# The recurrence's small inverse as its own chain, a few rows at a time, its first step tied behind eight VectorE instructions; u and v in one tile a head

## Chip, core and metric

The kernel runs on one core of a Trainium2 chip. The metric is the device time of one execution in microseconds (us), taken as the median of several runs. A profiled execution gives the trace that this document reads. The engines are called as the profile does: PE (TensorE, matrix products), PEld (its weight loads), DVE (VectorE), ACT (ScalarE), POOL (GpSimd) and SP (SyncE, which issues nearly all transfers here).

## What is computed

Two stacks of two layers each. A layer of the first stack has a mixer of three branches (a multi-scale pool, a differential attention, a two-way recurrence), gates, an output product and an MLP; the second stack has three kinds of attention. The change concerns only the recurrence of the first stack:

```python
def wkv7_scan(r, w, k, v, kk, a, reverse):
    def step(state, inp):
        r_t, w_t, k_t, v_t, kk_t, a_t = inp
        sa = einsum('bhij,bhj->bhi', state, -kk_t)
        state = (state * w_t[:, :, None, :] + sa[..., None] * (kk_t * a_t)[:, :, None, :]
                 + v_t[..., None] * k_t[:, :, None, :])
        return state, einsum('bhij,bhj->bhi', state, r_t)
    ...
y = direction(0, False) + direction(1, True)
```

There are 8 heads of 64 features, 512 steps and two directions. The kernel computes the scan in chunks of 64 steps. Within a chunk the steps hang together by a triangular 64x64 matrix for each head, direction and chunk, which has to be inverted.

## The kernel before

**Stages.** In each of the two layers of the first stack, `mixer` interleaves four generators. `rwkv_prepare` works through 4 pairs of heads; for each pair `rwkv_pair` makes the projections, and for each half of the sequence `rwkv_stage` makes the decayed keys and the masked products `scr` (L746 on PE, L748 on DVE), the transposed keys `bt` and the tile `uv`. So there are 8 stages a layer, 16 in all, and each ends in one inverse; they are called chain 1 to chain 16 here. `rwkv_recur` runs the chunks with what the stages left. `others` makes the pool and attention branches, and `gates` the gate products. Most of PE's time goes to products of the last two and of the projections: each is 24 matmuls 128x512 at L95 (`mm3`), whose weights are loaded to `wraw` and split by ACT (`whi`, L73) and DVE (`wlo`, L75).

**The inverse.** The four 32x32 diagonal blocks go by SP from `scr` to DRAM (`nd`, L782) and back, spread over the partitions, into `cN` (L789). Then come 31 steps of forward substitution on DVE, each a product into `cT` (L793) and a subtraction from `cX` (L795), 62 instructions in a row of dependences, and one negation (L796). `cX` goes to DRAM (`nx`, L797) and from there to its place in `scr` (L800). `rwkv_merge` adds the off-diagonal block: DVE transposes to `xz` (L813), PE multiplies twice (L816 and L823) with a copy by ACT between (L818). `cN`, `cX` and `cT` have one buffer each.

**The chunks.** `rwkv_chunks` makes for each chunk `px` (L837, L845), `xs` (ACT), `pu` (L854), then u, whose upper half ACT writes (L856) and whose lower half DVE writes (L857) into the same tile `uv`, then `pu` again (L862) and the next state `hist` (DVE, L869 or L872).

**What sets the order.** `Weave` holds the generators as chains with a priority and a time at which they are due, and lets the due one with the smallest number go on to its next `yield`, whose figures say how much PE time the piece is reckoned to fill and how long the chain then rests (1.8 times the second figure). The recurrence has priority 0, the preparation 1, the attention pieces 2, the other branches 3, the gates 4. The whole inverse is written out at the end of `rwkv_stage` in one piece; the merge is added as a chain of priority 0.2, due 60 of the planner's microseconds later:

```python
wv.add(0.2, self.rwkv_merge(rp, 2 * p + g, st, blocks, (sc, ar, bt, uv, pe)), 60.0)
```

A scheduler of the build then sets the final order on each engine's queue from what is written and from its own reckoning; that order is shown below where it matters. Each queue is worked off in that order.

Of the kernel before, what the change touches and what calls it, by code (L numbers as in the profile page):

```python
# [10 lines left out]
AF = mybir.ActivationFunctionType  # L11
ALU = mybir.AluOpType
# [3 lines left out]
P = 128  # L16
# [13 lines left out]
class B:  # L30
# [20 lines left out]
    def dump(self, name, ap):  # L51
        if self.dbg is not None and name in self.dbg:
            self.nc.gpsimd.dma_start(self.dbg[name], ap)


# [152 lines left out]
class First:  # L208
# [476 lines left out]
    def rwkv_stage(self, l, p, g, rp, wag, krkk, vv, st, wv):  # L685


        b, nc, pr = self.b, self.nc, self.pr
# [17 lines left out]
        for d in range(2):  # L706
            i = 4 * d + p
# [50 lines left out]
        yield 1.0, 0.0  # L758
        uv = b.t(rp, [P, 2, 2, 4, 64], "uv", bufs=2)
        nc.gpsimd.memset(uv[0:64, 0], 0.0)  # L760
        nc.gpsimd.memset(uv[64:P, 1], 0.0)
        ps = b.t(pr, [P, 2, 4, 64], "sc")
# [6 lines left out]
        for hh in range(2):  # L769
            nc.scalar.activation(out=uv[hss[1 - hh], hh], in_=ps[hss[1 - hh]], func=AF.Copy)  # L770
        yield 0.9, 0.0
# [8 lines left out]
        for h in range(2):  # L780
            for q in range(2):
                nc.sync.dma_start(nd[8 * h : 8 * h + 8, q].rearrange("n s t -> s n t"), blocks(h, q, q))  # L782
        N = b.t(rp, [P, 32, 32], "cN")
        X = b.t(rp, [P, 8, 32], "cX")
        tmp = b.t(rp, [P, 8, 32], "cT")
        nc.gpsimd.memset(X, 0.0)
        for e in range(4):
            nc.gpsimd.memset(X[32 * e : 32 * e + 32].rearrange("p i t -> p (i t)")[:, e::36], -1.0)
        nc.sync.dma_start(N.rearrange("p s t -> p (s t)"),  # L789
                          nd.rearrange("n q s t -> (n q) (s t)").unsqueeze(0).to_broadcast([4, 32, 1024]))  # L790
        for s_ in range(31):
            ni, nt = s_ // 4 + 1, 31 - s_
            nc.vector.tensor_tensor(out=tmp[:, :ni, :nt], in0=X[:, :ni, s_ : s_ + 1].to_broadcast([P, ni, nt]),  # L793
                                    in1=N[:, s_ : s_ + 1, s_ + 1 :].to_broadcast([P, ni, nt]), op=ALU.mult)
            nc.vector.tensor_tensor(out=X[:, :ni, s_ + 1 :], in0=X[:, :ni, s_ + 1 :], in1=tmp[:, :ni, :nt], op=ALU.subtract)  # L795
        nc.vector.tensor_scalar(out=X, in0=X, scalar1=-1.0, scalar2=None, op0=ALU.mult)  # L796
        nc.sync.dma_start(nx.rearrange("n q i e t -> e (n q) i t"), X)  # L797
        for h in range(2):
            for q in range(2):
                nc.sync.dma_start(blocks(h, q, q), nx[8 * h : 8 * h + 8, q].rearrange("n i e t -> (i e) n t"))  # L800
        wv.add(0.2, self.rwkv_merge(rp, 2 * p + g, st, blocks, (sc, ar, bt, uv, pe)), 60.0)

    def rwkv_merge(self, rp, i, st, blocks, parts):
# [8 lines left out]
        for h in range(2):  # L812
            nc.vector.transpose(out=xz[lo[h]], in_=blocks(h, 0, 0))  # L813
        for n in range(8):
# [14 lines left out]
    def rwkv_chunks(self, rp, g, hist, sc, ar, bt, uv, pe):  # L829
# [4 lines left out]
        for d in range(2):  # L834
            for c in range(4):
                for hh, hs in enumerate(hss):
                    nc.tensor.matmul(px[hs, d, c, :], lhsT=sc[:, d, c, hh, 0:64], rhs=uv[:, hh, d, c, :],  # L837
                                     start=(d == 0 and c == 0), stop=True, skip_group_check=True)
        yield 1.0, 0.0
        for c in range(4):  # L840
# [11 lines left out]
            for d in range(2):  # L852
                for hh, hs in enumerate(hss):
                    nc.tensor.matmul(pu[hs, 0, d, :], lhsT=sc[hs, d, c, hh, 0:64], rhs=xs[hs, d, :],  # L854
                                     start=(d == 0), stop=True, skip_group_check=True)
            nc.scalar.activation(out=uv[0:64, 0, :, c, :], in_=pu[0:64, 0], func=AF.Copy, scale=-1.0)  # L856
            nc.vector.tensor_scalar(out=uv[64:P, 1, :, c, :], in0=pu[64:P, 0], scalar1=-1.0, scalar2=None, op0=ALU.mult)  # L857
            yield 0.35, 0.7

            for d in range(2):  # L860
                for hh, hs in enumerate(hss):
                    nc.tensor.matmul(pu[hs, 1, d, :], lhsT=bt[:, hh, d, c, :], rhs=uv[:, hh, d, c, :], start=False, stop=True, skip_group_check=True)  # L862
            if cc:
# [11 lines left out]
    def rwkv_out(self, g, i, hist, y, st, sc, ar, bt, uv, pe):  # L875

        nc, b, pr = self.nc, self.b, self.pr
        hss = [slice(64 * hh, 64 * hh + 64) for hh in range(2)]
        for d in range(2):
            py = b.t(pr, [P, 4, 64], "sc")  # L880
            for c in range(4):
                for hh, hs in enumerate(hss):
                    nc.tensor.matmul(py[hs, c, :], lhsT=uv[:, hh, d, c, :], rhs=sc[:, d, c, hh, 64:P],
                                     start=(c == 0), stop=True, skip_group_check=True)
            for c in range(4):
                cc = 4 * g + c
                if cc:
                    for hs in hss:
                        nc.tensor.matmul(py[hs, c, :], lhsT=hist[hs, cc - 1, d, :], rhs=ar[hs, d, c, 64:P], start=False, stop=True, skip_group_check=True)
            nc.scalar.activation(out=y[:, d, 256 * g : 256 * g + 256].rearrange("p (c t) -> p c t", t=64), in_=py, func=AF.Copy)  # L890
            if not d:
                yield 1.1, 0.0
        st["done", i] = 1
        yield 1.1, 0.0
# [919 lines left out]
```

## Time and profile before

| | before |
|---|---|
| median of 3 runs | 3659.78 us (3654.95 to 3664.11) |
| profiled execution, its own time | 3664.09 us |
| span of its trace | 3662.3 us |
| PE busy | 3432.6 us, 94% of the span |
| DVE busy | 1888.0 us, 52% |
| ACT, POOL busy | 1221.1 us (33%), 552.2 us (15%) |
| mean granted PE clock | 0.968 |
| mixer of layer 0, mixer of layer 1 | about 90 to 700 us, 1200 to 1850 us |

A row of the page or of a wait table reads engine, line, operation, what it writes and reads, its form and how often, and behind the bar busy time and idle time ahead of it with what ended that. A busy PE is not a PE at its peak, since its matmuls overlap: a matmul 128x512 shows a duration of some 0.39 us while the next one starts 0.23 us after it.

### The profile page before, as it was taken

The page shows a single profiled execution, that of the slowest core. Times are in us where ns is not written, and L with a number is a line of the kernel's source. Part 1 is how long each engine was busy: PE and PEld are TensorE (multiplying, and loading weights), DVE is VectorE, ACT ScalarE, POOL GpSimd, SP SyncE. Part 2 cuts the span into 40 slices and gives each one's busy share as a digit, 9 for nine tenths or more (in the row PEclk, how much of TensorE's full clock was granted, in tenths as well). Part 3 has the DMA queues.
Part 4 walks back from the last instruction along what each step waited for, and adds up shares of the span by engine and source line. Part 5 has one row for each costly group of instructions (what it writes and reads, how often), then busy time and mean ns, then how long its engine had stood idle before and what let it go on. Part 6 is the DMA issues. An engine that isn't in the chain of part 4 may idle for free. (4 is left out here: it accounts for less than half of the span.)

```text
span 3662.3 us, 56248 instructions
## 1 busy us (share of the span) xinstructions
PE 3432.6 (94%) x22346; PEld 2748.1 (75%) x22346; DVE 1888.0 (52%) x4547; ACT 1221.1 (33%) x2339; POOL 552.2 (15%) x660
## 2 busy tenths in 40 slices
PE   7898989989999998989989999899999999999998
PEld 5666767678887666666768888888989978787777
DVE  6547666452235556566544234565465344645634
ACT  2233433222223333333222223344333234443423
POOL 2111211122201211111022210210000111100011
PEclk9899999999999998989999999999999999999999
DMA  5332223333333232222342335222222322222232
GB/s 176 84 83 73 62 70 95 101 119 98 92 94 128 82 92 68 65 69 69 104 142 70 98 92 147 48 42 62 63 68 70 87 73 59 54 57 70 70 92 92
DMA packets 471831, 309.37 MB, mean 84 GB/s; under 512 B 105084, under 2 KB 433796, under 8 KB 471568
## 3 DMA queue, kind: packets, MB, share of 16 engines
q1 hardware_dynamic: 470992, 303.68, 29.7%
q8 instruction: 176, 2.88, 0.3%
q0 software_dynamic: 576, 2.10, 0.1%
q14 instruction: 87, 0.71, 0.1%
HBM read 280.76 MB, written 24.95 MB: 83 GB/s over the span
## 5 line engine op out<-in xcount | busy, mean ns | idle before, releaser
L95 PE MATMUL mm<-xh,whi 128*128 128x512 f32 (+2 forms) x3024 | 1007.8, 364 | 32.9 <-DVE cX L795 26.4
L95 PE MATMUL mm<-xh,wlo 128*128 128x512 f32 (+2 forms) x3024 | 973.2, 353 | 8.5 <-DVE wlo L75 7.2
L95 PE MATMUL mm<-xl,whi 128*128 128x512 f32 (+2 forms) x3024 | 973.9, 353 | 0.0
L75 DVE TENSOR_TENSOR wlo<-wraw,whi 128x1024 fp32r<-128x1024 f32 (+3 forms) x454 | 529.0, 1165 | 607.9 <-ACT whi L73 593.4
L73 ACT ACTIVATE whi<-wraw 128x1024 fp32r<-128x1024 f32 (+2 forms) x466 | 452.5, 971 | 1107.1 <-PE mm L95 846.2
L95 PEld LDWEIGHTS mm<-xh,whi 128*128 128x128 f32 x3024 | 543.4, 192 | 134.9 <-issue 51.4
L95 PEld LDWEIGHTS mm<-xh,wlo 128*128 128x128 f32 x3024 | 540.4, 192 | 89.7 <-DVE wlo L75 10.9
L95 PEld LDWEIGHTS mm<-xl,whi 128*128 128x128 f32 x3024 | 541.2, 192 | 74.9 <-issue 8.9
L1276 ACT ACTIVATE s<-s,nm 128x256 f32<-128x256 f32 (+5 forms) x216 | 116.2, 539 | 184.8 <-DVE nm L1274 182.9
L793 DVE TENSOR_TENSOR cT<-cX,cN 128x60 f32<-128x60 f32 (+24 forms) x496 | 113.3, 229 | 114.2 <-DMA cN<-nd 88.8
L95 PE MATMUL mm<-yh,whi 128*128 128x512 f32 (+1 forms) x480 | 160.1, 368 | 7.4 <-ACT yh L108 4.1
L1054 PE MATMUL b<-whi,hh 128*128 128x512 f32 x416 | 164.6, 396 | 0.4 <-DVE PT L314 0.4
L1054 PE MATMUL b<-whi,hl 128*128 128x512 f32 x416 | 164.5, 395 | 0.0
L1054 PE MATMUL b<-wlo,hh 128*128 128x512 f32 x416 | 164.5, 395 | 0.0
L95 PE MATMUL mm<-yl,whi 128*128 128x512 f32 (+1 forms) x480 | 156.1, 358 | 3.3 <-DVE yl L109 3.3
L95 PE MATMUL mm<-yh,wlo 128*128 128x512 f32 (+1 forms) x480 | 154.0, 353 | 0.0
L1042 POOL TENSOR_TENSOR hid<-r 128x512 f32<-128x512 f32 x64 | 102.2, 1597 | 268.9 <-ACT r L1041 268.9
L109 DVE TENSOR_TENSOR hl<-hid,hh 128x512 fp32r<-128x512 f32 x64 | 43.3, 691 | 164.1 <-ACT hh L108 164.1
L795 DVE TENSOR_TENSOR cX<-cX,cT 128x60 f32<-128x60 f32 (+24 forms) x496 | 113.4, 229 | 10.6
L95 PEld LDWEIGHTS mm<-yh,whi 128*128 128x128 f32 x480 | 83.7, 189 | 28.2 <-ACT yh L108 7.0
L108 ACT ACTIVATE hh<-hid 128x512 fp32r<-128x512 f32 x64 | 39.3, 629 | 191.2 <-PE b L1054 184.4
L1310 DVE TENSOR_TENSOR y<-at,zs 128x128 f32<-128x128 f32 (+2 forms) x120 | 31.2, 263 | 138.9 <-PE at L1307 138.2
(377 smaller groups left out, 5108.9 us busy)
## 6 DMA issues: line engine op xcount, KB each, us to landing
wraw<-in_w_in_dram SPq DMA_DIRECT2D x228, 512.0 KB
wraw<-in_w_up_dram SPq DMA_DIRECT2D x64, 512.0 KB
wraw<-in_w_down_dram SPq DMA_DIRECT2D x64, 512.0 KB
wraw<-in_w_branch_dram SPq DMA_DIRECT2D x48, 512.0 KB
wraw<-in_w_out_dram SPq DMA_DIRECT2D x32, 512.0 KB
g<-acc SPq DMA_DIRECT2D x32, 256.0 KB
cN<-nd SPq DMA_DIRECT2D x16, 512.0 KB
th<-g SPq DMA_DIRECT2D x32, 256.0 KB
```

The lines of the kernel that those rows point to most:

```text
L73: self.nc.scalar.activation(out=wh, in_=rv, func=AF.Copy)
L75: eng.tensor_tensor(out=wl, in0=rv, in1=wh.bitcast(F32), op=ALU.subtract)
L95: self.nc.tensor.matmul(ps, lhsT=wt[:, k, :], rhs=xt[:, k, cs], start=(start and k == 0 and j == 0), stop=(k == nk - 1 and j == 2), skip_g ...
L108: nc.scalar.activation(out=hi, in_=ps, func=AF.Copy)
L109: nc.vector.tensor_tensor(out=lo, in0=ps, in1=hi.bitcast(F32), op=ALU.subtract)
L793: nc.vector.tensor_tensor(out=tmp[:, :ni, :nt], in0=X[:, :ni, s_ : s_ + 1].to_broadcast([P, ni, nt]), in1=N[:, s_ : s_ + 1, s_ + 1 :].to_b ...
L795: nc.vector.tensor_tensor(out=X[:, :ni, s_ + 1 :], in0=X[:, :ni, s_ + 1 :], in1=tmp[:, :ni, :nt], op=ALU.subtract)
L1042: nc.gpsimd.tensor_tensor(out=hidden(m), in0=r, in1=r, op=ALU.mult)
L1054: nc.tensor.matmul(ps[tt, n], lhsT=x[:, tk], rhs=y[:, 0, ns], start=(k == 0 and j == 0), stop=(k == FF - 1 and j == 2))
L1276: nc.scalar.activation(out=ss[i][:n, :nk], in_=ss[i][:n, :nk], func=AF.Exp, bias=nm[:n, i : i + 1], accum_out=sm[:n, i : i + 1])
L1310: nc.vector.tensor_tensor(out=y[:, c], in0=o[:, c.start - P * j : nq], in1=zs[:, c], op=ALU.mult)
```

## The change

1. The inverse leaves `rwkv_stage` and becomes the generator `rwkv_inverse`, a chain of its own with priority 0.2, due 17 of the planner's microseconds after the stage. It yields after every fourth step (rest 1.4), so that it is written out in eight pieces.
2. A stage waits with its `cN` transfer until the chain before it is written out (`("inv", i - 1)`); then it writes the transfer and adds the chain.
3. `b.pin` ties an instruction behind the last eight that were written for the same engine before it (an order alone, no semaphore). The first step of each chain is tied so, and the two transposes of each merge.
4. The merge is due 9 after the chain's end, where it was 60 after the stage's.
5. `uv` is two tiles, one a head, so that ACT's and DVE's halves of u are no longer writes to one tile.

The instructions are the same in kind and number on every engine; only their order and their waits differ.

```diff
+    def pin(self, ins, n=8):
+        found = 0
+        for i in reversed(self.nc.cur_bb.bb.instructions):
+            if i is not ins.ins and i.engine == ins.ins.engine:
+                self.tc.add_manual_dep(
+                    ins.ins, i.name, mybir.DependencyInfo(mybir.DependencyClass.NoSync, mybir.DependencyReason.DATA), reason="pin"
+                )
+                found += 1
+                if found == n:
+                    break
...
-        uv = b.t(rp, [P, 2, 2, 4, 64], "uv", bufs=2)
+        uv = [b.t(rp, [P, 2, 4, 64], f"uv{hh}", bufs=2) for hh in range(2)]
...
+        i = 2 * p + g
+        if i:
+            yield lambda: ("inv", i - 1) in st
         N = b.t(rp, [P, 32, 32], "cN")
+        nc.sync.dma_start(N.rearrange("p s t -> p (s t)"),
+                          nd.rearrange("n q s t -> (n q) (s t)").unsqueeze(0).to_broadcast([4, 32, 1024]))
+        wv.add(0.2, self.rwkv_inverse(rp, i, st, wv, blocks, N, nx, (sc, ar, bt, uv, pe)), 17.0)
+
+    def rwkv_inverse(self, rp, i, st, wv, blocks, N, nx, parts):
...
+            if s_ == 0:
+                b.pin(ins)
             nc.vector.tensor_tensor(out=X[:, :ni, s_ + 1 :], in0=X[:, :ni, s_ + 1 :], in1=tmp[:, :ni, :nt], op=ALU.subtract)
+            if s_ % 4 == 3:
+                yield 0.0, 1.4
...
-        wv.add(0.2, self.rwkv_merge(rp, 2 * p + g, st, blocks, (sc, ar, bt, uv, pe)), 60.0)
+        st["inv", i] = 1
+        wv.add(0.2, self.rwkv_merge(rp, i, st, blocks, parts), 9.0)
...
-            nc.vector.transpose(out=xz[lo[h]], in_=blocks(h, 0, 0))
+            b.pin(nc.vector.transpose(out=xz[lo[h]], in_=blocks(h, 0, 0)))
...
-            nc.scalar.activation(out=uv[0:64, 0, :, c, :], in_=pu[0:64, 0], func=AF.Copy, scale=-1.0)
-            nc.vector.tensor_scalar(out=uv[64:P, 1, :, c, :], in0=pu[64:P, 0], scalar1=-1.0, scalar2=None, op0=ALU.mult)
+            nc.scalar.activation(out=uv[0][0:64, :, c, :], in_=pu[0:64, 0], func=AF.Copy, scale=-1.0)
+            nc.vector.tensor_scalar(out=uv[1][64:P, :, c, :], in0=pu[64:P, 0], scalar1=-1.0, scalar2=None, op0=ALU.mult)
```

What moves is seen on two queues. The first place is DVE's queue in layer 0 from the end of chain 1 (the negation of `cX`) to the start of chain 2 (`cT` written 128x31). The number behind a name tells one buffer's use from another's; `zk` is a projection on its way out of PSUM. Before:

```order
L796 TENSOR_SCALAR cX_840<-cX_840 128x256
L75 TENSOR_TENSOR wlo_1282<-wraw_1279,whi_1281 128x1024
L390 SCALAR_TENSOR_TENSOR zk_1240<-mm_1215,PT_76,zk_1240 128x511
L793 TENSOR_TENSOR cT_1112<-cX_1111,cN_1110 128x31
L392 SCALAR_TENSOR_TENSOR zk_1240<-mm_1215,PT_76,zk_1240 128x511
L795 TENSOR_TENSOR cX_1111<-cX_1111,cT_1112 128x31
L813 STREAM_TRANSPOSE xz_1482<-scr_634 32x256
```

The same place after the change, where the lines have moved down (L796 is now L820, L75 is L87, L390 and L392 are L402 and L404, L510 is L522, L793 is L813, L795 is L817, L813 is L838, L857 is L882, L872 is L897). The negation that ends chain 1 stands three rows ahead of the first row shown, with two more `wlo` between:

```order
L87 TENSOR_TENSOR wlo_1363<-wraw_1360,whi_1362 128x1024
L522 SCALAR_TENSOR_TENSOR s_229_1299<-s_228_1295,s_224_1285 128x512
L87 TENSOR_TENSOR wlo_1485<-wraw_1482,whi_1484 128x1024
L402 SCALAR_TENSOR_TENSOR zk_1334<-mm_1309,PT_76,zk_1334 128x511
L404 SCALAR_TENSOR_TENSOR zk_1334<-mm_1309,PT_76,zk_1334 128x511
L838 STREAM_TRANSPOSE xz_1338<-scr_634 32x256 x2
L87 TENSOR_TENSOR wlo_1566<-wraw_1563,whi_1565 128x1024
L402 SCALAR_TENSOR_TENSOR zr_1457<-mm_1366,PT_76,zr_1457 128x511
L404 SCALAR_TENSOR_TENSOR zr_1457<-mm_1366,PT_76,zr_1457 128x511
L882 TENSOR_SCALAR uv_151_806<-pu_1417 64x2x64
L897 TENSOR_SCALAR hist_272<-pu_1417,pe_655 128x64 x2
L813 TENSOR_TENSOR cT_1437<-cX_1436,cN_1262 128x31
```

Between the end of one chain and the start of the next stood two instructions and stand now fifteen, among them five `wlo`, the merge's transposes and the first chunk of the recurrence.

The second place is PE's queue at the merge of chain 2: the merge's first product (`sc` from `xz` and `scr`), what stands between, and its second. Before:

```order
L816 MATMUL sc_1671<-xz_1670,scr_916 32x32 x16
L515 MATMUL at_1692<-s_258_1530,pw_1532 128x512
L854 MATMUL pu_1697<-xs_1668,scr_634 64x64 x4
L95 MATMUL mm_1637<-xh_69,whi_1633 128x512
L95 MATMUL mm_1637<-xl_70,whi_1633 128x512
L95 MATMUL mm_1637<-xh_69,wlo_1634 128x512
L95 MATMUL mm_1637<-xh_69,whi_1633 128x512
L95 MATMUL mm_1637<-xl_70,whi_1633 128x512
L95 MATMUL mm_1637<-xh_69,wlo_1634 128x512
L862 MATMUL pu_1697<-uv_805,bt_784 64x64 x4
L823 MATMUL sc_1722<-scr_916,xz_1670 32x32 x16
```

After the change (L816 is now L841, L823 is L848, L95 is L107, L422 is L434, L447 is L459); the first of the merge's sixteen 32x32 products stands two rows ahead of the first row shown:

```order
L107 MATMUL mm_1865<-xh_69,whi_1861 128x512
L107 MATMUL mm_1865<-xl_70,whi_1861 128x512
L107 MATMUL mm_1865<-xh_69,wlo_1862 128x512
L107 MATMUL mm_1865<-xh_69,whi_1861 128x512
L434 MATMUL at_1852<-ident_63,yo_1828 128x128 x4
L459 MATMUL at_1929<-kh_1723,qh_1625 128x512
L459 MATMUL at_1929<-kl_1724,qh_1625 128x512
L841 MATMUL sc_1831<-xz_1830,scr_842 32x32 x15
L459 MATMUL at_1929<-kh_1723,ql_1626 128x512
L107 MATMUL mm_1865<-xl_70,whi_1861 128x512
L459 MATMUL at_1930<-kh_1723,qh_1625 128x512
L848 MATMUL sc_1872<-scr_842,xz_1830 32x32 x16
```

One product of the merge now stands ahead of the other fifteen, with a few large ones between, and three large matmuls stand between the merge's two halves, where two groups of the recurrence and seven large ones stood.

## Rows read from the trace of the kernel before

**Rows 1.** The page's first part, the whole execution: busy time, share of span, instructions.

```profile
PE 3432.6 (94%) x22346; PEld 2748.1 (75%) x22346; DVE 1888.0 (52%) x4547; ACT 1221.1 (33%) x2339; POOL 552.2 (15%) x660
```

**Rows 2.** Busy time by stretch, us: PE, PEld, DVE, ACT, POOL, then PEclk, DMA share, GB/s.

```profile
90.00:700.00 610.00, 549.43 (x4355) 407.38 (x4354) 365.05 (x1067) 205.19 (x418) 98.75 (x169) 0.94 0.30 82
...
1200.00:1850.00 650.00, 587.78 (x4493) 432.04 (x4492) 386.19 (x1095) 213.61 (x434) 107.57 (x179) 0.93 0.29 80
...
1950.00:3662.30 1712.30, 1668.09 (x10572) 1405.68 (x10572) 824.51 (x1955) 612.44 (x1234) 209.06 (x191) 0.99 0.28 75
```

**Rows 3.** PE's waits, 90 to 700 us: waiter <- releaser, total us, times, longest.

```profile
PE mm L95 <- DVE cX L795: 10.8, 2, 9.8
PE pu L862 <- DVE uv L857: 8.0, 5, 3.6
PE at L447 <- DVE yo L483: 6.8, 1, 6.8
...
PE sc L906 <- DVE cT L793: 4.1, 2, 2.9
PE mm L95 <- DVE zk L392: 3.6, 1, 3.6
PE sc L746 <- DVE cX L795: 3.3, 1, 3.3
```

**Rows 4.** PE's waits, 1200 to 1850 us.

```profile
PE mm L95 <- DVE cX L795: 15.6, 2, 9.0
PE at L482 <- DVE s L479: 10.2, 2, 7.4
...
PE at L447 <- DVE mx L450: 5.1, 2, 4.4
...
PE at L447 <- DVE yo L483: 1.9, 1, 1.9
```

**Rows 5.** The instructions on tile cN: what DVE sat idle for, us, times.

```profile
  DMA cN<-nd: 88.8, 14
  POOL cX L788: 15.3, 2
```

**Rows 6.** DVE in order of time, start of chain 2: start us, duration, idle before.

```profile
158.53 0.19 DVE L793 TENSOR_TENSOR cT<-cX,cN 128x31 f32<-128x31 f32 x1 [11.63 <-DMA cN<-nd]
158.64 0.74 DVE L392 SCALAR_TENSOR_TENSOR zk<-mm,PT,zk 128x511 f32<-128x511 f32 x1
```

**Rows 7.** PE in order of time at the same place.

```profile
159.53 0.77 PE L95 MATMUL mm<-xh,whi 128*128 128x512 f32 x1 [9.85 <-DVE cX L795]
```

**Rows 8.** SP's issues at the same place: start us, us that the issue took.

```profile
143.13 3.95 SPq L789 DMA_DIRECT2D cN<-nd  x1
```

**Rows 9.** The L95 matmuls alone, ahead of that wait and after it: PE, PEld, PEclk.

```profile
138.60:149.20 10.60, 10.60 (x47) 8.60 (x46) 1.00 0.46 124
159.50:165.10 5.60, 5.57 (x13) 4.45 (x14) 0.50 0.02 4
```

**Rows 10.** DVE in order of time, end of chain 16 and its merge's first transpose.

```profile
1781.19 0.29 DVE L796 TENSOR_SCALAR cX<-cX 128x256 f32<-128x256 f32 x1
...
1789.10 0.43 DVE L813 STREAM_TRANSPOSE xz<-scr 32x256 f32<-32x256 f32 x1 [6.48 <-DMA scr<-nx]
```

**Rows 11.** The page's groups of the chains' steps, all sixteen chains.

```profile
L793 DVE TENSOR_TENSOR cT<-cX,cN 128x60 f32<-128x60 f32 (+24 forms) x496 | 113.3, 229 | 114.2 <-DMA cN<-nd 88.8
...
L795 DVE TENSOR_TENSOR cX<-cX,cT 128x60 f32<-128x60 f32 (+24 forms) x496 | 113.4, 229 | 10.6
```

**Rows 12.** DVE's waits, 90 to 1850 us.

```profile
DVE uv L857 <- ACT uv L856: 61.5, 25, 7.3
```

**Rows 13.** PE in order of time, the two halves of the merge of chain 1.

```profile
190.80 0.69 PE L816 MATMUL sc<-xz,scr 32*32 32x32 f32 x32
...
194.41 0.69 PE L823 MATMUL sc<-scr,xz 32*32 32x32 f32 x32
```

**Rows 14.** The instructions on tile xz: ACT's copies between the halves, ns least/median/most.

```profile
L818 ACT ACTIVATE xz<-sc x32: 374/376/380, 191.5 to 1820.6; 32x256 f32<-32x256 f32 x32
```

More of the change, by code (lines that the diff above doesn't have):

```diff
@@ L758, in rwkv_stage @@
         yield 1.0, 0.0
-        uv = b.t(rp, [P, 2, 2, 4, 64], "uv", bufs=2)
-        nc.gpsimd.memset(uv[0:64, 0], 0.0)
-        nc.gpsimd.memset(uv[64:P, 1], 0.0)
+        uv = [b.t(rp, [P, 2, 4, 64], f"uv{hh}", bufs=2) for hh in range(2)]
+        nc.gpsimd.memset(uv[0][0:64], 0.0)
+        nc.gpsimd.memset(uv[1][64:P], 0.0)
         ps = b.t(pr, [P, 2, 4, 64], "sc")
@@ L769, in rwkv_stage @@
         for hh in range(2):
-            nc.scalar.activation(out=uv[hss[1 - hh], hh], in_=ps[hss[1 - hh]], func=AF.Copy)
+            nc.scalar.activation(out=uv[hh][hss[1 - hh]], in_=ps[hss[1 - hh]], func=AF.Copy)
         yield 0.9, 0.0
@@ L782, in rwkv_stage @@
                 nc.sync.dma_start(nd[8 * h : 8 * h + 8, q].rearrange("n s t -> s n t"), blocks(h, q, q))
+        i = 2 * p + g
+        if i:
+            yield lambda: ("inv", i - 1) in st
         N = b.t(rp, [P, 32, 32], "cN")
+        nc.sync.dma_start(N.rearrange("p s t -> p (s t)"),
+                          nd.rearrange("n q s t -> (n q) (s t)").unsqueeze(0).to_broadcast([4, 32, 1024]))
+        wv.add(0.2, self.rwkv_inverse(rp, i, st, wv, blocks, N, nx, (sc, ar, bt, uv, pe)), 17.0)
+    def rwkv_inverse(self, rp, i, st, wv, blocks, N, nx, parts):
+        b, nc = self.b, self.nc
         X = b.t(rp, [P, 8, 32], "cX")
@@ L788, in rwkv_stage @@
             nc.gpsimd.memset(X[32 * e : 32 * e + 32].rearrange("p i t -> p (i t)")[:, e::36], -1.0)
-        nc.sync.dma_start(N.rearrange("p s t -> p (s t)"),
-                          nd.rearrange("n q s t -> (n q) (s t)").unsqueeze(0).to_broadcast([4, 32, 1024]))
         for s_ in range(31):
             ni, nt = s_ // 4 + 1, 31 - s_
-            nc.vector.tensor_tensor(out=tmp[:, :ni, :nt], in0=X[:, :ni, s_ : s_ + 1].to_broadcast([P, ni, nt]),
+            ins = nc.vector.tensor_tensor(out=tmp[:, :ni, :nt], in0=X[:, :ni, s_ : s_ + 1].to_broadcast([P, ni, nt]),
                                     in1=N[:, s_ : s_ + 1, s_ + 1 :].to_broadcast([P, ni, nt]), op=ALU.mult)
+            if s_ == 0:
+                b.pin(ins)
             nc.vector.tensor_tensor(out=X[:, :ni, s_ + 1 :], in0=X[:, :ni, s_ + 1 :], in1=tmp[:, :ni, :nt], op=ALU.subtract)
+            if s_ % 4 == 3:
+                yield 0.0, 1.4
         nc.vector.tensor_scalar(out=X, in0=X, scalar1=-1.0, scalar2=None, op0=ALU.mult)
@@ L836, in rwkv_chunks @@
                 for hh, hs in enumerate(hss):
-                    nc.tensor.matmul(px[hs, d, c, :], lhsT=sc[:, d, c, hh, 0:64], rhs=uv[:, hh, d, c, :],
+                    nc.tensor.matmul(px[hs, d, c, :], lhsT=sc[:, d, c, hh, 0:64], rhs=uv[hh][:, d, c, :],
                                      start=(d == 0 and c == 0), stop=True, skip_group_check=True)
@@ L861, in rwkv_chunks @@
                 for hh, hs in enumerate(hss):
-                    nc.tensor.matmul(pu[hs, 1, d, :], lhsT=bt[:, hh, d, c, :], rhs=uv[:, hh, d, c, :], start=False, stop=True, skip_group_check=True)
+                    nc.tensor.matmul(pu[hs, 1, d, :], lhsT=bt[:, hh, d, c, :], rhs=uv[hh][:, d, c, :], start=False, stop=True, skip_group_check=True)
             if cc:
@@ L882, in rwkv_out @@
                 for hh, hs in enumerate(hss):
-                    nc.tensor.matmul(py[hs, c, :], lhsT=uv[:, hh, d, c, :], rhs=sc[:, d, c, hh, 64:P],
+                    nc.tensor.matmul(py[hs, c, :], lhsT=uv[hh][:, d, c, :], rhs=sc[:, d, c, hh, 64:P],
                                      start=(c == 0), stop=True, skip_group_check=True)
```

## Prediction

> **What bounds the kernel now.** I read the page's first part first: PE is busy 94% of the span, the next engine 52% [rows 1]. So the time is PE's work, plus PE's idle time, plus what a lower clock makes of the work. Then the stretches: in the two mixers, which alone contain what the change touches, PE is busy 549.4 of 610 and 587.8 of 650 us, so it idles 60.6 and 62.2 us there, and its mean granted clock is 0.94 and 0.93; in the second stack it idles 44 us of 1712 at 0.99 [rows 2]. What the change can give or take is in those 123 us of idle time and in the clock.
>
> Who ends PE's waits? Nearly always DVE [rows 3, 4]. The releasers have different names, but the place is mostly one: DVE stands still at the first step of a chain, and what PE needs is queued behind it. At chain 2 SP issues the transfer to `cN` at 143.13 [rows 8]; DVE reaches the first step and idles 11.63 us, until 158.53; right behind that step stands L392, which frees a PSUM tile [rows 6]; PE waits 9.85 us and goes on at 159.53 [rows 7]. All sixteen chains do this: 88.8 + 15.3 = 104.1 us of DVE's idle time [rows 5]. PE feels part of it, since it has work of its own. I looked at what DVE did during each of PE's longer waits; those that begin while DVE stands at a first step are 10.8 + 6.8 + 4.1 + 3.6 + 3.3 = 28.6 us in layer 0 [rows 3] and 15.6 + 7.4 + 4.4 + 1.9 = 29.3 us in layer 1 (of two of those rows only the longest wait) [rows 4]: **58 us**, about half of the mixers' idle time.
>
> Such a wait costs more than itself. Ahead of it 47 matmuls took 10.6 us, 0.23 us each, at clock 1.00 (2.4 GHz); behind it 13 took 5.6 us, 0.43 us each, at 0.50 (1.2 GHz) [rows 9]. The mixers' clock lies 0.05 and 0.06 below that of the second stack, which is 0.05 x 610 + 0.06 x 650 = 70 us of full rate [rows 2]. The 58 us are 0.47 of the mixers' idle time, so 33 us of the 70 go with them. Some of the half-rate time lies in the waits themselves and costs nothing; I take 0.7 of it, **23 us**, bounds 0 and 33.
>
> **The change part by part.**
>
> *Removed: the waits at the chains' first step.* The pin, the later due time and the wait for the chain before put DVE work ahead of that step, mostly `wlo` splits, each of which waits until PE has done a product of 24 matmuls and freed a weight buffer: 24 x 0.23 = 5.5 us each [rows 9]. In the order I counted for each chain the PE work that must be done between SP's `cN` transfer and DVE's reaching of the first step, at 0.23 us a large matmul and the small ones at their spacing in the trace: before 0 to 8.3 us, after 12.0 to 33.2 us. The transfer took 15.4 us at chain 2, the longest of the sixteen [rows 6, 8]. Thirteen chains have 14.9 us or more, as much as that or within half a microsecond of it; three (chains 1, 5 and 9, with 12.0 to 13.6) could wait some 3 us each, which I price at nothing since these are first chains of a pair, where no other transfer of a chain is in flight; 10 us is the bound. So I take the whole 58 and the 23. The later `cN` transfers and `nx` stand on SP's queue with weight loads behind them; in the order each of these loads may still be issued 12 us of PE work or more ahead of its use, with nearly the same spread before and after, so this costs nothing unless a transfer takes more than that. POOL's memsets of `cX` move with the chain, to where the transfer they wait for is over, and POOL is 15% busy [rows 1]: nothing.
>
> *Added: waits at the merges.* Here the trace of before shows no case, as PE had 21 to 44 us of work between the point where a chain can end and the merge's first product. After the change it has 7.6 to 27 us. What it needs: from the end of chain 16 (1781.19 + 0.29) to the first transpose, which waited for the transfers, 7.6 us [rows 10], and two transposes of 0.43, so 8.5 us, with a hand-over some 8.6. To this comes how far DVE is behind PE when the chain ends. A chain's own steps are (113.3 + 113.4) / 16 = 14.2 us [rows 11], the PE work beside them 12 us at least, so an estimate of the lag starts near 2 us where the chain is alone; splits and softmax rows between the steps make it more; I take 3.5. With 12.1 us needed, seven merges fall short (they have 9.4, 10.5, 11.7, 9.1, 10.6, 9.9 and 7.6), together 16 us; for the scatter of the lag I take **20 us**, and 20 x 23 / 58 = **8 us** of clock. The ends: without lag only the chain with 7.6 us falls short, 1 us; with a lag of 10 us thirteen do, together 85 us. I take a value near the low end because DVE's idle time at the first step, which made it late before, is gone. While PE waits there, everything behind the merge on its queue waits too, and with the pinned transposes so do `wlo` and the chunks' `uv` and `hist` on DVE.
>
> The Trainium skill has a shorter way for the transfers: its page "DMA: Bandwidth & Descriptors", section "Anatomy of one DMA — SWDGE (gpsimd) path", fits 2.0 us plus the bytes at 436 GB/s for a transfer (one that POOL issues, while SP issues these), by which the two in a row here (128 and 32 KB) would land after an estimated 4.4 us. This trace has 7.6 us [rows 10]; the measurement decides, and by the page the term of the merges would be 1 or 2 us.
>
> *Added: the gap inside a merge.* Between the end of a merge's first half and the second PE had 194.41 - 191.49 = 2.9 us [rows 13], and it needs ACT's two copies of 0.376 us [rows 14] and two hand-overs, about 1.1 us. After the change three large matmuls, 0.7 us, often stand between: 0.4 us x 16 = **6 us**, bounds 0 and 10.
>
> *Removed: the tie between the halves of u.* DVE waited 61.5 us for ACT's half [rows 12], most of it time in which it had nothing else to do; PE waited 8.0 us for DVE's half [rows 3], partly because of the chains. I take **4 us**, bounds 0 and 8.
>
> Sum: -58 - 23 + 20 + 8 + 6 - 4 = **-51 us**. The profiled execution took 3664.09 us, 4.3 more than the median of the runs; 3664 - 51 - 4 = **3609 us**, 1.4% less. Next late after this are the waits that the nine rows leave: in the chunks and the attention, and the new ones at the merges.
>
> **The rivals.**
>
> *A: the merges take it back.* The wait moves from DVE's queue, where PE felt half of it, to PE's own queue, where it feels all of it. With a lag of 7.5 us the merges fall short by some 55 us, and with clock (22) and the gaps (6) this equals the 81 + 4 that goes: no change, about 3658. For it: in the order the first product of a merge is drawn ahead of its fifteen others, so it stands about where the scheduler reckons the transposes to be over, and its reckoning of the `cN` transfer was short by up to 11.63 us [rows 6]. Against it: the count above.
>
> *B: slower.* The same mechanism with a lag of 10 us in every chain: 85 us of waits and 85 x 23 / 58 = 34 of clock, with 6 for the gaps against 85 removed: +40, about 3700. It decides from a lag of some 7.5 us. For it: chains in the attention's stretch share DVE with up to 63 other instructions. Against it: in before DVE came to its work soon after PE except behind a first step.
>
> *C: the merges wait for nothing.* If DVE keeps level with PE, their term is 1 us, with no clock: -58 - 23 + 1 + 6 - 4 = -78, about 3582. The page named above would give the same, as its transfers are shorter. For it: PE has other short waits, which give DVE time; against it, rows 10.
>
> *D: the first steps still wait.* Should SP come late to the `cN` transfer, because `nx` ahead of it waits for a chain's end, only the clock and some of the 58 go. Against it: this order, `nx` ahead of `cN`, was there before too, and its 15.4 us were counted in.
>
> **How the numbers follow.** Forecast, with merge waits between about 8 and 45 us: 0.59. C: 0.13. A, with D's milder form: 0.13. B and what ends like it: 0.15. What a measurement of this kernel can tell from no change is 0.3%, 11 us: 3649 to 3671. Faster 0.59 + 0.13 = 0.72, same 0.13, slower 0.15. The range: the low end is all bounds of the gain, 3664 - 58 - 33 - 8 + 1 - 4 = 3562, taken to 3566; the upper reaches over most of A, to 3656, and leaves B out.
>
> **What would show it.** Right: in the profile after, DVE's idle time for `cN` falls from 104 us to under 15; PE's rows of L95, L447, L482 and L906 waiting for DVE shrink by some 50 us; PE idles some 90 us in the two mixers instead of 123; the clock there is 0.95 or more; a new row appears, the merge's first product waiting for `xz`, of some 20 us. Wrong: that row shows 50 us or more (A, B) or is missing (C), or DVE still idles for `cN` (D). The forecast is also wrong if the mixers' other waits, on which I put no change, grow by 30 us, as the order of everything between moves too.

## The result, and the profile after

The changed kernel takes **3614.96 us** (median of 4 runs, 3612.24 to 3617.68) where the kernel before takes 3657.64 us beside it (4 runs, 3654.95 to 3664.11): a ratio of 0.9881, 95% interval 0.9864 to 0.9898, so 1.2% faster. Its profiled execution took 3614.28 us, 49.8 us less than the profiled one of before; the forecast was 51 us less. By the medians it is 42.7 us less, as the profiled execution of before lies 6.4 us above its median.

The page's first part, and its two groups of the chains' steps (engine line, busy us, mean ns, behind the second bar idle us ahead of them):

```profile
PE 3430.6 (95%) x22346; PEld 2747.3 (76%) x22346; DVE 1891.6 (52%) x4547; ACT 1220.2 (34%) x2339; POOL 559.2 (15%) x660
...
L817 DVE TENSOR_TENSOR cX<-cX,cT 128x60 f32<-128x60 f32 (+24 forms) x496 | 110.0, 222 | 12.1
L813 DVE TENSOR_TENSOR cT<-cX,cN 128x60 f32<-128x60 f32 (+24 forms) x496 | 109.5, 221 | 11.8
```

PE's work is the same as in [rows 1]. The step groups kept their 220 ns, but the idle time ahead of the first of them, 114.2 us with 88.8 for `cN` in [rows 11], is 11.8 us, and no part of it is for `cN`: the view of the instructions on tile `cN`, which in [rows 5] named 104.1 us of DVE's idle time, names nothing any more.

To compare the mixers I cut both traces at the same work: from the first masked product of a layer (`sc<-ar,bk`) to the first transpose behind its mixer (`xtok` or `htok`). Busy time by stretch of **before**, then of **after** (length, then PE, PEld, DVE, ACT, POOL; then PEclk, DMA share, GB/s):

```profile
90.40:787.80 697.40, 623.84 (x4717) 463.44 (x4717) 409.63 (x1121) 227.70 (x446) 122.82 (x184) 0.94 0.32 89
1233.60:1933.10 699.50, 625.75 (x4691) 461.04 (x4691) 407.85 (x1119) 224.48 (x443) 120.52 (x180) 0.93 0.31 87
```

```profile
90.30:763.70 673.40, 624.96 (x4716) 464.33 (x4716) 411.78 (x1121) 226.49 (x446) 124.85 (x184) 0.95 0.33 93
1209.50:1881.80 672.30, 621.42 (x4690) 458.40 (x4690) 409.98 (x1119) 224.92 (x443) 124.80 (x180) 0.94 0.32 91
```

The two mixers together went from 1396.9 to 1345.7 us, -51.2; all else moved by 1.4 us. PE ran the same matmuls in them: its busy time fell from 1249.6 to 1246.4 us and its idle time from 147.3 to 99.3 us. So **48 of the 51 us are idle time** and 3 are the clock. (The stretches of [rows 2] show the idle time as 41.5 and 50.9 us, but hold more work now, since everything behind them comes earlier.)

PE's waits in the stretches of [rows 3] and [rows 4], after (waiter <- releaser, us, times, longest):

```profile
PE sc L841 <- DVE xz L838: 16.1, 7, 5.3
PE at L494 <- DVE s L491: 8.5, 4, 3.8
PE sc L758 <- DVE scr L760: 4.5, 4, 2.2
```

```profile
PE sc L841 <- DVE xz L838: 10.8, 3, 7.4
PE mm L107 <- DVE wlo L87: 7.3, 1, 7.3
PE at L494 <- DVE s L491: 6.6, 3, 2.3
...
PE pu L887 <- DVE uv L882: 0.4, 1, 0.4
```

The long rows behind the chains' first step (the weight products behind `cX`, the attention's products, the chunks' products behind `cT`) are gone or small. In their place stands the row that the prediction named: the merge's first product waits for `xz`, 26.9 us in ten merges. One wait is new and was not in the prediction, 7.3 us for `wlo`. At the start of chain 2, which stood for all chains in [rows 6 to 8], DVE now comes to the first step from other work, with `cN` long there; DVE and SP in order of time:

```profile
174.39 0.47 DVE L897 TENSOR_SCALAR hist<-pu,pe 128x64 f32<-128x64 f32 x2 [0.91 <-PE pu L887]
174.78 0.18 DVE L813 TENSOR_TENSOR cT<-cX,cN 128x31 f32<-128x31 f32 x1
```

```profile
140.22 0.56 SPq L799 DMA_DIRECT2D cN<-nd  x1
140.83 0.54 SPq L821 DMA_DIRECT2D nx<-cX  x1
```

The transfer is issued at 140.22 and needed 34.6 us later.

### The profile page after: what moved, and what is told of

It reads as the page before. It is cut to its first block, busy times and chain, and to the rows that moved or that the text cites. A ratio compares the mean times of both kernels' runs of the same rounds, so it can differ in the third digit from the quotient of the medians.

```text
span 3612.5 us, 56238 instructions
## 1 busy us (share of the span) xinstructions
PE 3430.6 (95%) x22346; PEld 2747.3 (76%) x22346; DVE 1891.6 (52%) x4547; ACT 1220.2 (34%) x2339; POOL 559.2 (15%) x660
## 5 line engine op out<-in xcount | busy, mean ns | idle before, releaser
L107 PE MATMUL mm<-xh,whi 128*128 128x512 f32 (+2 forms) x3024 | 1002.9, 362 | 2.9 <-ACT whi L85 1.7
L107 PE MATMUL mm<-xh,wlo 128*128 128x512 f32 (+2 forms) x3024 | 969.4, 352 | 8.7 <-DVE wlo L87 7.3
L107 PE MATMUL mm<-xl,whi 128*128 128x512 f32 (+2 forms) x3024 | 972.7, 353 | 0.0
L87 DVE TENSOR_TENSOR wlo<-wraw,whi 128x1024 fp32r<-128x1024 f32 (+3 forms) x454 | 526.2, 1159 | 648.3 <-ACT whi L85 609.0
L107 PEld LDWEIGHTS mm<-xh,whi 128*128 128x128 f32 x3024 | 540.9, 191 | 102.2 <-issue 23.5
L107 PEld LDWEIGHTS mm<-xh,wlo 128*128 128x128 f32 x3024 | 537.6, 191 | 85.8 <-DVE wlo L87 8.7
L107 PEld LDWEIGHTS mm<-xl,whi 128*128 128x128 f32 x3024 | 538.5, 191 | 72.6 <-issue 7.1
L1301 ACT ACTIVATE s<-s,nm 128x256 f32<-128x256 f32 (+5 forms) x216 | 116.2, 539 | 184.7 <-DVE nm L1299 180.3
L107 PE MATMUL mm<-yh,whi 128*128 128x512 f32 (+1 forms) x480 | 160.4, 368 | 10.0 <-ACT yh L120 5.3
L107 PE MATMUL mm<-yl,whi 128*128 128x512 f32 (+1 forms) x480 | 155.1, 356 | 4.9 <-DVE yl L121 4.9
L107 PE MATMUL mm<-yh,wlo 128*128 128x512 f32 (+1 forms) x480 | 154.0, 353 | 0.0
L817 DVE TENSOR_TENSOR cX<-cX,cT 128x60 f32<-128x60 f32 (+24 forms) x496 | 110.0, 222 | 12.1
L813 DVE TENSOR_TENSOR cT<-cX,cN 128x60 f32<-128x60 f32 (+24 forms) x496 | 109.5, 221 | 11.8
L107 PEld LDWEIGHTS mm<-yh,whi 128*128 128x128 f32 x480 | 84.2, 190 | 31.4 <-issue 7.7
L890 POOL TENSOR_TENSOR hp<-hist,pe 128x128 f32<-128x128 f32 x56 | 37.8, 675 | 432.3 <-DVE hist L894 185.7
```

The costliest lines, as they stand in the source:

```text
L87: eng.tensor_tensor(out=wl, in0=rv, in1=wh.bitcast(F32), op=ALU.subtract)
L107: self.nc.tensor.matmul(ps, lhsT=wt[:, k, :], rhs=xt[:, k, cs], start=(start and k == 0 and j == 0), stop=(k == nk - 1 and j == 2), skip_g ...
L813: ins = nc.vector.tensor_tensor(out=tmp[:, :ni, :nt], in0=X[:, :ni, s_ : s_ + 1].to_broadcast([P, ni, nt]), in1=N[:, s_ : s_ + 1, s_ + 1 : ...
L890: nc.gpsimd.tensor_tensor(out=hp, in0=hist[:, cc - 1], in1=pe[:, :, c : c + 1].to_broadcast([P, 2, 64]), op=ALU.mult)
L1301: nc.scalar.activation(out=ss[i][:n, :nk], in_=ss[i][:n, :nk], func=AF.Exp, bias=nm[:n, i : i + 1], accum_out=sm[:n, i : i + 1])
```

## The experiments

The theory (T1): the gain is DVE's wait for `cN`, taken away because the tie and the new order put other work ahead of the first step; part of it comes back at the merges. The rivals: the uv tiles carry the gain (R1); cutting the chain in pieces carries it (R2); the tie isn't needed, earlier issue and pieces do it (R3). All times are medians, beside a before of 3652 to 3658 us. The last three columns are us in the two mixers, cut as above, of one profiled execution each: PE idle, PE busy, and the time at the lower of TensorE's two levels (1.2 GHz), summed from the clock record of the trace.

| kernel | us | ratio to before, 95% | PE idle | PE busy | at 1.2 GHz |
|---|---|---|---|---|---|
| before | 3657.64 | | 147 | 1250 | 191 |
| after | 3614.96 | 0.9881 (0.9864-0.9898) | 99 | 1246 | 143 |
| uv in one tile | 3614.98 | 0.9895 (0.9879-0.9910) | 99 | 1241 | 126 |
| first step untied | 3654.03 | 1.0003 (0.9993-1.0013) | 126 | 1256 | 181 |
| one piece | 3750.1 | 1.0258 (1.0240-1.0275) | 165 | 1317 | 304 |
| one piece, merge due 40 | 3631.3 | 0.9942 (0.9926-0.9958) | 118 | 1245 | 164 |
| merge due 18 | 3594.04 | 0.9837 (0.9824-0.9850) | 83 | 1247 | 123 |
| merge due 18, two cX | 3604.01 | 0.9867 (0.9848-0.9885) | 87 | 1251 | 133 |
| merge due 24 | 3603.07 | 0.9867 (0.9851-0.9883) | 89 | 1243 | 140 |
| pieces of two rows | 3591.65 | 0.9838 (0.9816-0.9860) | 84 | 1238 | 119 |
| due 18, pieces of two | 3578.69 | 0.9800 (0.9786-0.9815) | 80 | 1231 | 116 |
| ... and first step untied | 3643.56 | 0.9970 (0.9957-0.9984) | 117 | 1247 | 154 |
| ... and MEMSET tied | 3567.85 | 0.9766 (0.9745-0.9786) | 73 | 1224 | 96 |
| after, MEMSET tied | 3616.85 | 0.9884 (0.9862-0.9906) | 100 | 1256 | 164 |

**The uv tiles.** The chunk's two halves of u go back into one tile:

```diff
-        uv = [b.t(rp, [P, 2, 4, 64], f"uv{hh}", bufs=2) for hh in range(2)]
+        uvt = b.t(rp, [P, 2, 2, 4, 64], "uv", bufs=2)
+        uv = [uvt[:, hh] for hh in range(2)]
```

> The kernel after, with u and v of both heads again in one tile; the order of the instructions is unchanged. Theory T1 (the gain of 43 us is DVE's wait for cN at the first steps, taken away by the order; the uv tiles are worth a few us): +1 to +8 us on 3615, so 3616 to 3623; PE's rows of px and pu waiting for the DVE write of uv go from 1.2 back to about 9 us in the two mixers. Rival R1 (the tiles carry the gain): at least +25, 3640 or more.

3614.98 us, the time of after. PE's waits in both mixers:

```profile
PE sc L842 <- DVE xz L839: 24.6, 11, 7.2
PE pu L888 <- DVE uv L883: 1.2, 3, 0.5
```

The row for `uv` stays at 1.2 us: R1 falls, and my own +1 to +8 with it. PE's wait for DVE's half of u (8.8 us in before) does not come from the shared tile alone. But the two tiles did not part the halves either: in before, in after and in this run DVE's write waits for ACT in all 64 cases and never starts before ACT's has ended, 0.03 us behind it at the least. So no run here prices halves that are really apart. Both also read the same `pu`; whether that ties them was not tried.

**The tie.** The first step loses its tie, and nothing else changes:

```diff
-            if s_ == 0:
-                b.pin(ins)
```

> The kernel after without the tie of the chain's first step; pieces, merge due times and tiles stay. By the order the TensorE work between the cN transfer's issue and the first step shrinks from 12 to 33 us to 3 to 11 us, as it was in the kernel before (0 to 8), and one merge instead of seven has less than 12.1 us behind its chain's end. T1: DVE is idle for cN for 80 to 105 us again (after: 0), PE idles some 50 us more for the chains' DVE results, the merges wait some 20 us less: 3640 to 3660. Rival R3 (the early issue and the pieces do it, the tie is not needed): 3610 to 3620 with under 20 us of DVE idle for cN.

3654.03 us: the whole gain is gone, and R3 falls. What DVE idled for on tile `cN` (us, times), then two of PE's waits in both mixers:

```profile
  DMA cN<-nd: 57.9, 13
  POOL cX L810: 7.9, 1
```

```profile
PE pu L885 <- DVE uv L880: 21.9, 7, 5.3
...
PE sc L839 <- DVE xz L836: 7.8, 5, 2.8
```

The waits are those of T1, in other sizes and partly at other rows: DVE idles for the first steps 65.8 us where I had put 80 to 105, and PE's idle time is up 27 us, not 50, with 10 us more of busy time. The merges give back 19 us as expected, and the wait for `uv` is back at 21.9 us with two tiles.

Do PE's waits come from DVE's standing at the first steps? Many of them end some us after it. The trace can be followed back: from each of PE's waits for DVE in the mixers to the DVE instruction that ended it, and from there through DVE's unbroken work to the idle time ahead of it. PE's waits that lead to a first step's wait for `cN` or `cX` so sum to 68.7 us in before, to 0 in after and to 44.8 without the tie (19.6 of the 21.9 for `uv` among them; in before 2.3 of the 8.8). Less the 19 us that the merges give back, 44.8 leaves 26, nearly the 27 us of idle time that came back. The ties of the merges' transposes were left in place in every run, and the tie alone in the order of before was not tried.

**One piece.** The inverse is written out in a row, still tied:

```diff
-            if s_ % 4 == 3:
+            if s_ > 31:
                 yield 0.0, 1.4
```

> The kernel after with the inverse's 62 DVE steps and 31 rows written out in one piece behind the tied first step. By the order cN has 7 to 27 us of TensorE work ahead of the first step, and the merges 7 to 14 us behind the chain (after: 8 to 27). T1: DVE idle for cN of 5 to 25 us in place of 0, merges waiting 35 to 50 us in place of 27, and other PE work waiting behind the 62 steps in a row: 3625 to 3645. Rival R2 (the pieces carry the gain): 3650 or more with DVE idle for cN under 25 us.

3750.1 us, over 100 us more than T1 had, and with the marks of R2. The first steps are not the cause: DVE idles 2.1 us for `cN`. PE's busy time for the same matmuls is up by 71 us and its idle time by 66; the merges wait 53.7 us in place of 26.9:

```profile
PE sc L841 <- DVE xz L838: 53.7, 12, 8.8
```

Busy time by stretch shows the place, behind the merge of chain 4 (which starts at 357):

```profile
340.00:357.00 17.00, 14.18 (x68) 11.14 (x67) 9.31 (x36) 3.94 (x8) 1.83 (x7) 0.99 0.35 90
357.00:402.00 45.00, 38.18 (x370) 28.98 (x371) 15.23 (x32) 11.85 (x29) 6.50 (x12) 0.55 0.15 40
402.00:425.00 23.00, 16.72 (x74) 12.49 (x73) 16.88 (x44) 4.14 (x8) 5.43 (x7) 0.63 0.07 15
```

Ahead of it PE runs weight products at 0.99; behind it come 370 matmuls in 45 us, nearly all small ones, with gaps between, at 0.55. Without rests, I take it, the planner writes the chain, its merge and the chunks close behind each other, and PE gets stretches of small products with little that is large between. Is it then the piece, or the merge that follows too early? The same kernel with the merge due 40 (`9.0` to `40.0` in the line that adds it):

> The kernel after with the inverse in one piece behind the tied first step, as in the run that took 3750 us, but with the merge due 40 behind it instead of 9. By the order every merge has 14 to 41 us of TensorE work behind its chain (one piece and 9: 7 to 14), and the first steps 4 to 22 us, five of them under 6. Theory T1 (the loss of the one piece came from merges and their small products brought close behind each chain): the merges wait under 8 us in all, DVE is idle for cN for 15 to 35 us, the low-clock time of the two mixers falls from 304 to under 200 us, and the time to 3620 to 3655. Rival R2 (the steps in one row on DVE cost it, wherever the merge stands): 3700 or more.

3631.3 us: R2 falls in the form that it had (3700 or more), as the early merge made most of the loss. But against after with its pieces the one piece is still 16 us behind. DVE idles at the first steps again, though for another reason than I gave:

```profile
  POOL cX L810: 52.2, 6
  DMA cN<-nd: 1.3, 1
```

They are for POOL's MEMSET of `cX`; POOL in turn sat idle 180.3 us in all ahead of its MEMSETs, until `nx` of the chain before was over.

**The merge's due time**, which the row for `xz` asks for:

```diff
-        wv.add(0.2, self.rwkv_merge(rp, i, st, blocks, parts), 9.0)
+        wv.add(0.2, self.rwkv_merge(rp, i, st, blocks, parts), 18.0)
```

> The kernel after with the merge's due time 18 instead of 9 behind the inverse; nothing else. By the order every merge has 13 to 37 us of TensorE work behind its chain's end (after: 8 to 27, seven under 12.1), and the first steps keep 8 to 29 us. T1 with the transfers to the inverse and back as what the merges wait for: the row of PE at the merge's first product waiting for xz falls from 27 to under 6 us, and the time to 3588 to 3600. Rival (the merge's wait is only handed on, to the chunks behind the merges or the layer's end): 3610 to 3620.

3594.04 us, in the middle of T1's range, 21 us under after. The row for `xz` is down from 26.9 to 2.0 us; PE's idle time fell by 16:

```profile
PE sc L841 <- DVE xz L838: 2.0, 3, 1.3
```

So the merges' waits had to be paid for, and a due time gets most of it back. Later still does not help:

> The kernel after with the merge due 24 instead of 9 (18 gave 3594 us with no row of PE waiting for xz). T1 (only the merges' wait was to be had): 3589 to 3600, the same as 18, since no merge is short of what it needs but one (11 us). Rival A (every us of delay frees more): under 3587. Rival B (the chunks behind the merges run out of weight products at the layer's end, their last px comes 12 us of TensorE work later than with 18): over 3602, with the idle time of PE in the last 150 us of each mixer up by 8 or more.

3603.07 us, a figure that fits B, and so does the place: in the last 150 us of the two mixers PE's idle time is up by 4.2 and 3.4 us, more than all of the 6 us by which it grew, and the granted clock is lower there (0.92 to 0.84 and 0.94 to 0.89). The size is less than the 8 us that B asked for, and that weight products ran out is not shown. The row for `xz` came back as 12.7 us in thirteen short waits, but not for the transfers: at no merge does the first transpose wait. DVE comes to it from other work.

**Pieces of two rows**, with the merge due 18 and due 9:

```diff
-            if s_ % 4 == 3:
-                yield 0.0, 1.4
+            if s_ % 2 == 1:
+                yield 0.0, 0.7
```

> The kernel with the merge due at 18, with a piece of the inverse every two rows (priced 0.7 us) instead of every four (1.4 us). If what is left of PE's waits for DVE in the mixers (some 83 us idle) comes from other DVE results queued behind eight chain steps: 5 to 12 us less, 3582 to 3589. If those waits are for chains of other work (branch instructions, ACT): 3591 to 3597.

> The kernel after with a piece of the inverse every two rows instead of every four, and the merge's due time left at 9. By the order the TensorE work that the merges lack against 12.1 us sums to 10 us (after: 16; merge due at 18: 0). If pieces and merge time work apart and add up (with the merge at 18, two rows gave 15 us): 3597 to 3604 against 3615, PE waiting 12 to 25 us for xz. If the pieces only helped where the merge stood later: 3610 to 3618.

3578.69 and 3591.65 us: 15 us less with the merge at 18 where I had 5 to 12, and 23 less with it at 9 where I had 11 to 18; both lie below my ranges. With the merge at 9 the row for `xz` is 12.6 us, as expected. With it at 18 the mechanism is not mine: PE's idle time fell by 3 us, and the other 16 us are busy time of the same matmuls. The clock can be only part of that: PE's busy time at the lower level fell from 111 to 96 us, which at half the rate is worth an estimated 8 us. The masked products (`sc<-ar,bk`, L758) alone went from 58.4 to 46.5 us. I had no term for that, and why it is so stays open.

The tie once more, in the kernel with both (the same two lines taken out):

> The kernel with merge due 18 and pieces of two rows (3579 us), without the tie of the chain's first step. By the order the first steps have 0 to 11 us of TensorE work behind the transfer's issue (tied: 12 to 29). T1 (the tie takes away DVE's wait for cN, whatever the pieces and merges): DVE is idle for cN for 50 to 100 us again, 3610 to 3625. Rival R3 (finer pieces and later merges hide that wait as well): under 3590.

3643.56 us, 65 us more: R3 falls, and T1's 3610 to 3625 was too low by 19 us. The tie is worth more here than in after (39), though DVE's wait for `cN` is about that of the first untied kernel:

```profile
  DMA cN<-nd: 61.9, 14
```

Of the mixers' 53 us in the profiled execution (the fastest of the twelve), 37 are idle time and 16 busy time. Followed back as above, 29.7 us of PE's waits lead to a first step, where none did with the tie. Why the rest is lost is open.

**POOL's MEMSET.** Why does PE wait 7.3 us for `wlo` in after? Back through the trace, POOL, DVE, PE in order of time:

```profile
1261.92 4.33 POOL L515 TENSOR_TENSOR s<-s 128x526 f32<-128x526 f32 x3 [16.64 <-ACT s L510]
1274.95 0.31 POOL L808 MEMSET cX<- 128x256 f32 x1 [8.70 <-DMA nx<-cX]
1275.22 1.26 POOL L515 TENSOR_TENSOR s<-s 128x512 f32<-128x512 f32 x1
```

```profile
1277.44 0.69 DVE L522 SCALAR_TENSOR_TENSOR s<-s,s 128x512 f32<-128x512 f32 x1 [12.09 <-POOL s L520]
```

```profile
1279.32 0.79 PE L107 MATMUL mm<-xh,wlo 128*128 128x512 f32 x1 [7.31 <-DVE wlo L87]
```

The MEMSET stands amid the pool branch's work, waits 8.70 us for `nx` of chain 9, the pool branch's last part comes behind it, DVE waits 12.09 us for that, and `wlo` stands behind DVE's wait. The first attempt gave `cX` two buffers, in the kernel with the merge at 18:

```diff
-        X = b.t(rp, [P, 8, 32], "cX")
-        tmp = b.t(rp, [P, 8, 32], "cT")
+        X = b.t(rp, [P, 8, 32], "cX", bufs=2)
+        tmp = b.t(rp, [P, 80], "cT")
```

> The kernel with the merge due at 18 (3594 us), and two buffers for cX so that POOL's MEMSET of it need not wait for the transfer nx of the chain before; cT is packed into 80 elements a partition to make room. The order is that of merge 18. If the MEMSET's wait is what holds POOL's branch and behind it DVE's weight low part (PE wlo: 6.1 us at one place): that row goes and the time falls by 3 to 8 us, to 3586 to 3591. If it is hidden or the cause is another: 3592 to 3596 and the row stays.

3604.01 us, 10 more, which neither case had; PE's wait for `wlo` at this place is 6.7 us (6.1 without the second buffer). It tells nothing on the cause: with two buffers POOL's queue has the MEMSET of the chain after the next at the same place, waiting for the same transfer (8.07 us there). What the 10 us are stays open (the four runs go from 3594.73 to 3609.67). The second attempt ties the MEMSET behind the POOL work that is written ahead of it:

```diff
-        nc.gpsimd.memset(X, 0.0)
+        b.pin(nc.gpsimd.memset(X, 0.0))
```

> The kernel with merge due 18 and pieces of two rows (3579 us), with POOL's MEMSET of cX tied behind the eight POOL instructions ahead of it in the program, as the first step is on DVE; by the order it then stands behind the token mixer's tensor_tensor of s and not between them. If the wait of that MEMSET for the transfer nx is what makes DVE and PE wait at one place of the second mixer (6.2 us, PE for wlo): that row goes and the time falls to 3570 to 3575. If something else holds them: 3577 to 3581 with the row still there.

> The kernel after, with POOL's MEMSET of cX tied behind the eight POOL instructions ahead of it in the program and nothing else; this prices the term that the prediction set at nothing. If the MEMSET's wait for nx in the middle of the token mixer's tensor_tensor of s is what made DVE wait 12.1 us for s and PE 7.3 us for wlo at one place of the second mixer: both rows go and the time falls from 3615 to 3603 to 3609, the idle time of PE in the second mixer from 51 to 42 to 45 us. If other work takes its place: 3612 to 3618.

With merge 18 and pieces of two: **3567.85 us**, 11 less and 2 below the range, the fastest kernel here, 1.3% under after; the row for `wlo` is down from 6.6 to 0.4 us, 7 us are idle time, 7 more busy time in the profiled execution. In after alone: 3616.85 us (3602.49 to 3629.84, and the profiled one is the longest of them), no change that such a spread could tell. DVE's wait of 12.1 us for `s` and PE's for `wlo` are gone there too, but

```profile
PE sc L841 <- DVE xz L838: 36.8, 11, 7.9
```

the merges now wait 36.8 us in place of 26.9. In the second layer they wait 5.8 us more, 3.0 of it at chain 9, right behind the place, and PE's idle time there stayed at 51 us: most of what was freed was waited for again. The other 4.1 us stand in the first layer, ahead of the place, so they do not come from it. That the cure counts only where the merges have room fits the two runs; it is not shown by them.

## Why the prediction was right, step by step

**First steps, -58: right, the size a little low.** DVE's idle time for `cN` went to 0, under the 15 that I asked for. PE's rows that I had named (L95 behind `cX` 26.4, L447 18.8, L482 10.9, L906 4.1, L746 behind `cX` 3.8, L95 behind `zk` 3.6, together 67.6 us in the mixers) fell to 20.0 us, with the attention's row L494 still at 15.0: -48. Followed back through DVE, 68.7 us of PE's waits led to the first steps, and none does now. Taking the tie away brings the time back, and 44.8 us of such waits. What I had called the cause, the order ahead of the first step, is thereby shown.

**Clock, -23 and +8: mis-sized.** The time at 1.2 GHz did fall, from 191 to 143 us, but PE's busy time in the mixers fell by 3 us, not 15, and the clock there is 0.95 and 0.94 where I asked for 0.95 or more. (After and the run with uv in one tile, which has its order, differ by 6 us of busy time and 17 us at 1.2 GHz; so 3 us is nothing clear, and 15 would be.) I had priced the lost rate by the weight products alone [rows 9]. Of each matmul I count the time by which it lengthens PE's busy time. So counted, the `mm` products went from 746 to 737 us, of which 77 and 58 at the lower level. The merges' and chunks' small products took it back: `sc<-xz,scr` and `px<-uv,scr` together took 10.6 us more for the same count, 19 us of them now at the lower level where it had been under 1. A microsecond at the lower level did not cost the same everywhere: 3 us of busy time for 48 from before to after, 71 for 160 from after to the one piece. I have no rule for it.

**Merges, +20: nearly right in size, by a partly wrong working.** 26.9 us. I took 7.6 us for the transfers from chain 16 [rows 10] and 3.5 of lag. Chain 7 is the better example (SP, then DVE, then PE):

```profile
555.45 0.55 SPq L799 DMA_DIRECT2D cN<-nd  x1
556.11 0.54 SPq L821 DMA_DIRECT2D nx<-cX  x1
558.75 6.86 SPq L557 DMA_DIRECT2D g<-acc  x1
565.65 0.44 SPq L71 DMA_DIRECT2D wraw<-in_w_in_dram  x1
567.61 1.80 SPq L824 DMA_DIRECT2D scr<-nx  x4
```

```profile
570.37 0.90 DVE L838 STREAM_TRANSPOSE xz<-scr 32x256 f32<-32x256 f32 x2 [5.40 <-DMA scr<-nx]
```

```profile
570.95 0.28 PE L841 MATMUL sc<-xz,scr 32*32 32x32 f32 x2 [5.32 <-DVE xz L838]
```

The chain ends at 555.95; the transpose comes 14.4 us later. The long issue of `g` in between is over at 565.61 and does not hold `scr` up: `nx` itself lands only at 567.6, since POOL's MEMSET, which waits for it too, starts at 567.66. Where DVE had to wait at a merge, the way from the chain's end to the transpose is 13.4 to 14.4 us if the next chain's `cN` is issued close to `nx`, just ahead of it (chains 3, 5, 7) or between it and `scr` (chains 11, 13), and 6.5 to 9.2 us otherwise (7.6 in chain 15, whose next `cN` is issued 10 us behind `nx`). PE's waits at those five chains are 18.7 of the 26.9 us; 6.0 are at chains 1, 2 and 6, where DVE did not wait but came late.

Chain 16, from which I took the 7.6 us, has no chain behind it. The trace of before had shown the longer way: at its chains 3 and 9, with `cN` issued just ahead of `nx`, it took 12.0 and 12.3 us from the issue of `nx` to that of `scr`, and 4.7 to 6.8 at the others. I had weighed the place of `nx` on SP's queue for the first steps (rival D, which had `nx` always ahead of `cN`), and not that of `cN` for the merges. Some of the need was thus far above my 12.1 us and some below, and that the sum came out near is in part luck.

Rival C (3582) falls: ten merges waited. The page "DMA: Bandwidth & Descriptors" of the Trainium skill, by whose fit (section "Anatomy of one DMA — SWDGE (gpsimd) path") I had estimated 4.4 us, leads to C; the traces have 6.5 to 14.4. The same page, section "Two DMAs through the same engine are not ordered", says that within one queue of one DMA engine the descriptors start in order. The traces fit that: `nx` to `scr` took 11.5 us behind a `cN` at chain 7 and 4.7 us without one at chain 8; at chain 13, where `cN` stands behind `nx` and ahead of `scr`, that step took 4.7 us, and the 8.8 us from the issue of `scr` to the transpose are the long part. A kernel with the next `cN` behind both `nx` and `scr` at every chain was not tried.

**Gap inside the merge, +6:** PE itself did not wait for ACT's copy, its weight loads did for 3.9 us; in waits the term was at most that. **uv, -4: wrong.** The term took the halves to be parted by two tiles. They are not: DVE waits for ACT's half as before, and longer, 80.8 us in place of 61.5 [rows 12], while PE waits for DVE's half only 1.2 us:

```profile
DVE uv L882 <- ACT uv L881: 80.8, 29, 9.3
```

**POOL's memsets, nothing: wrong.** They do wait for `nx` where they stand now, and POOL's 15% said nothing on where; one of these waits cost PE 7.3 us. But with the MEMSET tied in after the time did not change, so the sum did not suffer.

The sum held because two errors cancelled, which is luck: the clock gave 12 us less than reckoned, and the idle time fell by 48 us where my waits sum to -36. By the way back through DVE the first steps gave 69 us of PE's waits, not 58, and the merges took 27, not 20. The other 7 us are mostly PE's waits for ACT and POOL, which fell from 17 to 6 us; I had no term for them and don't attribute them.

## What to carry to other kernels

Before a step that waits for a transfer, count the work that the other engines have between the transfer's issue and that step, in the final order: by my count the tie raised it from 3-11 us to 12-33 us, which took away 66 us of DVE's waiting and was worth 39 us here; in the better kernel it was 62 us of waiting and 65 us of time. Do the same count for every wait at the chain's end, and look at what is issued just ahead on the same queue. Where several waits lie in a row on the same work, removing one can feed the next: price a cure in the kernel in which it will run.

## What was not expected of the hardware

The same matmuls of the two mixers, 9,406 to 9,408 in each trace, kept PE busy for 1224 to 1317 us with 96 to 304 us at the lower level; what changed was their order and the waits between them, and two executions of one order differed by 6 us. A due time and the size of a piece, which change no instruction, moved the kernel between 3579 and 3750 us; in one of these steps (pieces of two, merge at 18) five sixths of the gain were busy time and not waits, of which the clock explains an estimated half.
